# Two more stages of a decoder layer in seven products: query and key of heads 0 to 7, and a fourth pair in the recurrent output

## The chip, the cores and the metric

The kernel runs on one core of a Trainium2 chip, in one launch. The metric is the device time of that core in microseconds (us), the median of repeated runs. The profiled execution is one such run, recorded with every instruction. TensorE multiplies matrices and writes PSUM (8 banks of 128 x 512 fp32 values here), VectorE and ScalarE work element by element, GpSimd (POOL) issues the loads that add into their target, and SyncE (SP) issues the plain loads and stores.

## The reference

One layer of a decoder, 256 tokens, width 2048, all float32. `x` is normed and projected by one wide matrix; a recurrent branch and a stick-breaking attention run side by side, are gated and merged, and a feed-forward part and a gated embedding follow:

```
h = rmsnorm(x, g_mix)
x_r, g_r, q, k, v, gate_r, gate_a = split(h @ w_in)
y_r = gelu(g_r) * rg_lru(conv(x_r))          # 2816 wide
y_r = y_r @ w_rnn_out                        # 2816 -> 2048
q, k = head_rmsnorm(q), head_rmsnorm(k)      # 16 heads of 128
y_a = stick_breaking_attention(q, k, v) @ w_attn_out
x = x + (sigmoid(gate_r) * y_r + sigmoid(gate_a) * y_a) @ w_o
g, u = split(rmsnorm(x, g_ffn) @ w_ffn_gu)
x = x + (silu(g) * u) @ w_ffn_down           # 5632 wide
x = x + sigmoid(rmsnorm(x, g_ple) @ w_ple_gate) * (p @ w_ple_proj)
```

## The kernel before

**Numbers in two parts.** TensorE is used in its fp32r format. To keep precision, each operand is split into a high part and the rest (`whi`, `wlo` for weights). ScalarE writes the high part (line 370) and VectorE the rest (line 371). A *product*, `prod` (lines 640 to 644), is three matmuls of 512 columns: high by high, high by rest, rest by high.

**Weights.** `plan` lists all weight tiles in the order of use, cut into chunks of up to 1024 columns (512 KB). `Stream` loads them (line 281, on SP's queue, in the fixed order `DMA_ORDER`, each load behind the one before), sums them where asked, and splits them (lines 370 and 371). Split weights have five buffers, raw plain ones four (`w`), and everything else that is 1024 columns wide shares 31 buffers, tag "Q": normed inputs, recurrent outputs, attention's tiles, and the raw weights that take part in sums. Tiles of 512 columns share 18 buffers, tag "H". `need` keeps the splits four chunks ahead of the product that uses them, and sums two chunks more.

**Groups.** Stages from the recurrent output on compute two 128-token halves by two column blocks of 512 at once. `group` (line 706) runs such a group through a list of *slots*. A number is a plain chunk, one contraction tile of 128: 4 products. The other slots form the seven-product scheme for 2 x 2 blocks (Strassen's, in Winograd's form) over pairs of contraction tiles: "11", "T1", "21", "T2", "22", "T3", "T4" serve pairs 0 and 1 together, and A1 to A4 and B1 to B4 (written ("S", i, p)) serve pairs 2 and 3. Over all its slots a pair takes 7 products where the plain form takes 8. `pairs_of` says how many pairs a stage has: four for those named in `FOUR`, else three (two in the short last down part). The weights' sums are made by VectorE (line 292) and by loads that add into a tile (`joins`, line 330, issued by POOL). The inputs' sums come from `half_sums`: four operations of 128 columns and one split.

At a slot `group` can also run other work. The call's `also` names functions by slot, the list `todo` gives one to each slot from the second on, and the list `pend` (transposes of the stage just done) gives one to each slot in `TURNED_AT`. `whole` runs a group and adds its banks to the evacuated tiles, with four VectorE additions at its end.

**Blocks.** The present query and key projections and the attention gate use `block` (line 849): 512 columns, 16 contraction tiles, both token halves, 32 products. Every second contraction tile it calls `step`, eight steps a block. A step is four products.

**The order around the change.** Recurrence (11 channel pairs), recurrent output (two groups, slots `LONG`), value (two groups, `EVEN4`), then eight blocks Q0, K0, Q1, K1, ... and four gate blocks, which make 96 steps. Behind each query or key block stands `head_norms` (line 980): squares on ScalarE, a norm, and the scaled heads on VectorE. Attention for a pair of heads `hp` has four parts: `att_t` turns query and key by eight transposes, `att_z` makes the logits, `att_e` the sums along the keys and the weights, `att_o` the output. They are issued at steps 18 + 9 hp plus 0, 2, 7 and 11. The value tiles of the second value group are split by `next_v` at steps 1, 3, 5 and 7. At steps 93 to 95 `parts_sums` makes the input sums of the attention output, which follows. In the end come three rounds of gated groups (`gu`) and down parts (`dn`). The last down part has two groups with the slots `TWELVE`, and the stage behind it, `pg`, reads their result turned by `next_h` (line 1179).

**Scheduling.** The program fixes the order on each engine when it is built, by priorities in the order of the code and a time model. Waits between engines are semaphores.

Of the kernel before, what the change touches and what calls it, by code (L numbers as in the profile page):

```python
# [32 lines left out]
A1, A2, A3, A4 = [("S", i, 2) for i in (1, 2, 3, 4)]  # L33
B1, B2, B3, B4 = [("S", i, 3) for i in (1, 2, 3, 4)]
FIRST3 = ["11", A1, 6, "T1", A2, 7, "T2", "21", "22", A3, "T3", 8, A4, 9, "T4", 10, 11, 12, 13, 14, 15]
EVEN3 = ["11", A1, 6, "T1", A2, 7, "21", 8, "T2", 9, "22", A3, 10, "T3", 11, A4, 12, "T4", 13, 14, 15]
EVEN4 = ["11", A1, 8, B1, "T1", 9, A2, B2, 10, "21", "T2", 11, "22", A3, 12, B3, "T3", 13, A4, B4, 14, "T4", 15]
LONG = ["11", 6, A1, 7, "T1", 8, A2, 9, "T2", 10, "21", 11, "22", 12, A3, 13, "T3", 14, A4, 15, "T4",
        16, 17, 18, 19, 20, 21]
TWELVE = [("S", 1, 0), ("S", 1, 1), 4, ("S", 2, 0), 5, ("S", 2, 1), 6, ("S", 3, 0), 7, ("S", 3, 1), 8, ("S", 4, 0), 9,  # L40
          ("S", 4, 1), 10, 11]
TWO = (0, 1)
FOUR = ("gu", "v")
LAST_GROUP = ("pg", 1)
W_BUFS = 4
RAW_AHEAD = 12.0
SUMS_AHEAD = 2
TURNED_AT = {"first": (5, 7, 9, 11), "twelve": (6, 8, 10, 12), "even": (9, 11, 13, 15)}
NEG = -1e30


def pairs_of(name):

    if name[:2] == "dn":
        q = int(name[2])
        return [FQ0[q] // 2 + i for i in range(3 if FQ[q] == 16 else 2)]
    return (0, 1, 2, 3) if name in FOUR else (0, 1, 2)


def is_sum(x):  # L60

    return isinstance(x, str) or isinstance(x, tuple) and x[0] == "S"
# [14 lines left out]
C_XR, C_GR, C_Q, C_K, C_V, C_GTR, C_GTA = 0, 22, 44, 60, 76, 92, 108  # L77
# [3 lines left out]
NPC = 226  # L81


ATT_AT = (0, 2, 7, 11)


def rg_k_tiles(j):
# [77 lines left out]
def tail():  # L165


    def wide(name, w, slots, c=0):
        return [(name, g, w, c + 8 * g, c + 8 * g + 4, slots[g]) for g in range(2)]

    def blocks(*cs):
        return [("blk", b, None, c, None, None) for c, b in cs]

    def gu(*gs):
        return [("gu", g, "gu", 4 * g, 44 + 4 * g, EVEN4 if g else FIRST3) for g in gs]

    def dn(q):
        k, p = FQ0[q], FQ0[q] // 2
        slots = [x + k if isinstance(x, int) else (*x[:2], x[2] + p) if isinstance(x, tuple) else x
                 for x in (EVEN3 if FQ[q] == 16 else TWELVE)]  # L180
        return wide(f"dn{q}", "dn", [slots] * 2)

    x = [("x", 0), ("x", 1)]
    return (wide("ro", "ro", [LONG] * 2) + wide("v", "in", [EVEN4] * 2, C_V)
            + blocks(*[(c, b) for b in range(4) for c in (C_Q, C_K)], *[(C_GTA, b) for b in range(4)])
            + wide("ao", "ao", [EVEN3] * 2) + wide("wo", "wo", [FIRST3, EVEN3]) + gu(0, 1, 2, 3) + dn(0) + gu(4, 5, 6, 7) + dn(1)
            + gu(8, 9, 10) + dn(2)
            + wide("pg", "pg", [FIRST3[:-4] + x + FIRST3[-4:]] * 2))
# [234 lines left out]
def tile_hybrid_block(ctx: ExitStack, tc: tile.TileContext, xT: bass.AP, x: bass.AP, pT: bass.AP,  # L423
# [12 lines left out]
    def tl(tag, dt=F32):  # L436
        cnt[0] += 1
        tag = "H" if tag in "CT" else "Q"
        n, c = NT[tag]
        return act.tile([P, c], dt, tag=tag, name=f"{tag}_{cnt[0]}", bufs=n)  # L440

    def psum():
        cnt[0] += 1
        return pps.tile([P, 512], F32, tag="ps", name=f"ps_{cnt[0]}")

    def f32(ap):
        return ap.bitcast(F32)

    def tt(o, a, b, op):
        nc.vector.tensor_tensor(o, a, b, op)  # L450

    def stt(o, a, s, b, op0, op1):
        nc.vector.scalar_tensor_tensor(o, a, s, b, op0, op1)

    def actv(o, i, f, **kw):
        nc.scalar.activation(o, i, f, **kw)  # L456
# [27 lines left out]
    def pc(base, j):  # L484
        return prm_sb[:, base + j:base + j + 1]
# [37 lines left out]
    def parts(t):  # L523
        v = t.rearrange("p (e x s) -> p e x s", e=2, x=2)
        return v[:, :, 0, :], v[:, :, 1, :]

    def pair(t):
        return t.rearrange("p (e s) -> p e s", e=2)
# [105 lines left out]
    pend, todo = [], []  # L634

    def tok(pairs, k, t):
        x = rhs(pairs, k)
        return x[:, t * P:t * P + P], x[:, 256 + t * P:384 + t * P]

    def prod(ps, x, wh, wl, start=False, stop=False, goes_on=False):  # L640

        nc.tensor.matmul(ps, x[0], wh, start=start, stop=False, skip_group_check=goes_on)  # L642
        nc.tensor.matmul(ps, x[0], wl, start=False, stop=False, skip_group_check=goes_on)  # L643
        return nc.tensor.matmul(ps, x[1], wh, start=False, stop=stop, skip_group_check=goes_on)  # L644
# [39 lines left out]
    xg = []  # L684
# [21 lines left out]
    def group(at, pairs, sums, after=None, also=()):  # L706
# [8 lines left out]
                 if isinstance(x, int) or is_sum(x)]  # L715
        turned_at = TURNED_AT["twelve" if len(slots) == len(TWELVE) else
                              "first" if slots[2] == 6 and slots[8] == "22" else "even"]
# [49 lines left out]
    xc, xcs, gel, y, gtr, ysum, xsum = {}, {}, {}, [], [], {}, {}  # L767
# [81 lines left out]
    def block(c0, b, step=None):  # L849

        pss = [psum() for _ in range(2)]
        wt = S_.take(("blk", c0, b))
        for k in range(KD):
            if step is not None and k % 2 == 0:
                step()
            _, _, hi, lo, o = wt[4 * k]
            for t, ps in enumerate(pss):
                prod(ps, tok(xg, k, t), hi[:, o:o + 512], lo[:, o:o + 512], k == 0, k == KD - 1)
        return pss

    def rs_x(t):
        return rstd_tok[:, t:t + 1]
# [7 lines left out]
    @contextmanager  # L870
    def behind_splits():
        with tc.issue_after(S_.hi_ins.ins), tc.issue_after(S_.lo_ins.ins):
            yield
# [15 lines left out]
    pss = group(("gtr", 0), xg, None, None, also)[0]  # L889
# [12 lines left out]
    for p in range(NPR):  # L902
# [14 lines left out]
        def step():  # L917
            if count[0] in (0, 2, 4, 5):
                with behind_splits(), tc.issue_after(gelu.ins):
                    next(parts_, None)  # L920
            count[0] += 1

        pss = block(C_GTR, GATE_R_AT[p], step)
# [5 lines left out]
    def whole(at, pairs, sums, also=()):  # L929

        (q2, q4, q3, q8), t = group(at, pairs, sums, None, also)
        cs = [t[y] for y in ("11", "T3", "T2", "T1")]
        for c, q in zip(cs, (q2, q4, q3, q8)):
            tt(c, q, c, ALU.add)
        return cs

    def parts_sums(pairs, sums, p):
        h = tl("T")
        hi, lo = parts(pairs[p])
        tt(pair(h), f32(hi), f32(lo), ALU.add)  # L940
        sums[p] = half_sums(h)
# [8 lines left out]

    n = len(LONG)
    for g in range(2):
# [9 lines left out]
    def next_v():  # L962
        c, r = vc.pop(0), rs_x(len(vs) % 2)
        v = tl("B", F32R)
        actv(v[:, :512], c, AF.Identity, scale=r)
        stt(v[:, 512:], c, r, f32(v[:, :512]), ALU.mult, ALU.subtract)
        vs.append(v)
# [5 lines left out]
    qs, ks, zst, ost = {}, {}, {}, []  # L973
# [3 lines left out]

    heads = {C_Q: {}, C_K: {}}

    def head_norms(c0, b, step):  # L980

        pss = block(c0, b, step)
        ss = stat.tile([P, 16], F32, tag="ss", name=f"ss_{c0}_{b}")
        for t, ps in enumerate(pss):
            q = tl("T")
            for h in range(4):
                actv(q[:, h * P:h * P + P], ps[:, h * P:h * P + P], AF.Square, scale=rs_x(t),
                     accum_out=ss[:, 4 * t + h:4 * t + h + 1])
        r = ss[:, 8:]
        rsqrt_mean(r, ss[:, :8], HD)  # L990
        for t, ps in enumerate(pss):
            nc.vector.tensor_scalar(r[:, 4 * t:4 * t + 4], r[:, 4 * t:4 * t + 4], rs_x(t), None, ALU.mult)
            c = tl("T")
            tt(c.rearrange("p (h d) -> p h d", h=4), ps.rearrange("p (h d) -> p h d", h=4),
               r[:, 4 * t:4 * t + 4].unsqueeze(2).to_broadcast([P, 4, P]), ALU.mult)
            heads[c0][b, t] = c
# [14 lines left out]
    def att_t(hp):  # L1011
        ks[hp] = turn_heads(C_K, hp, pc(PC_KG, 0))
        qs[hp] = turn_heads(C_Q, hp, qg)
# [73 lines left out]

    at = {}
    for hp in range(NHP):
        for d, f in enumerate(ATT_AT):  # L1090
            at.setdefault(18 + 9 * hp + f, []).append(((att_t, att_z, att_e, att_o)[d], hp))
    osum = {}
    for i, p in enumerate(pairs_of("ao")):
        at[93 + i] = [(lambda p: parts_sums(ost, osum, p), p)]
    slot = [0]

    def step():
        for f, hp in at.pop(slot[0], ()):
            f(hp)
        slot[0] += 1  # L1100

    for b in range(4):
        if b == 0:
            for i in range(4):
                at.setdefault(1 + 2 * i, []).append((lambda _: next_v(), 0))
        head_norms(C_Q, b, step)
        head_norms(C_K, b, step)
    gta = []
    for b in range(4):
        pss = block(C_GTA, b, step)  # L1110
# [87 lines left out]
    for g in range(2):  # L1198
# [5 lines left out]
        for n, ps in enumerate(group(("wo", g), mix, msum, onto_x1(g))[0]):  # L1204
            t, b = n % 2, 2 * g + n // 2
# [77 lines left out]
    for g in range(2):  # L1283
        qs_, t_ = group(("pg", g), h3, sum3, also={len(FIRST3) - 4: embedded(g)} | (
            {} if g else {10: lambda: token_scales(1, rs2)}))
        for n, (q, c) in enumerate(zip(qs_, ("11", "T3", "T2", "T1"))):
            t, b, op = n % 2, 2 * g + n // 2, ALU.add
            c, ps, o = t_[c], pp.pop(0), tl("T")
# [76 lines left out]
```

## Time and profile before

| | |
|---|---|
| median of 3 runs | 1856.9 us (1856.87 to 1857.93) |
| profiled execution | 1856.98 us, of which the span from first to last instruction is 1855.2 us |
| VectorE, ScalarE busy | 1499.7 us (81%), 1253.4 us (68%) |
| loaded | 409.11 MB, mean 221 GB/s |

The page gives busy times, the span in 40 slices, the chain of work that ended last, and groups of instructions by line. In a group's row, "| 851.6, 390 | 0.2 <-" means busy us in total, mean ns of one, and the idle time of the engine just before it with what ended it. In rows by time, the first two numbers are start and length in us, and a bracket gives the idle time before it and its releaser.

### The profile page before, as it was taken

What the parts mean: (1) busy time and instruction counts of PE and PEld (TensorE: products, weight loads), DVE (VectorE), ACT (ScalarE), POOL (GpSimd) and SP (SyncE); (2) the same over time, 40 slices, a digit from 0 to 9 for tenths busy, and PEclk for the clock granted to TensorE, in tenths of its full rate; (3) what the DMA queues carried; (4) which work ended last, traced back from release to release, by engine and by line L of the source; (5) the groups of instructions that cost most, each with busy time, mean ns of one, the idle gap of its engine ahead of it and who ended that gap; (6) DMA issues with size and microseconds to landing.
All of it is one profiled execution on the core that took longest, in us unless ns stands there. A gap on an engine that the chain in (4) does not pass through costs nothing.

```text
span 1855.2 us, 24724 instructions
## 1 busy us (share of the span) xinstructions
PE 1845.1 (99%) x8885; PEld 1552.7 (84%) x8885; DVE 1499.7 (81%) x1889; ACT 1253.4 (68%) x1679; POOL 115.9 (6%) x140
## 2 busy tenths in 40 slices
PE   9999999999999999999999999999999999999998
PEld 7899889888888888888888888888888888888787
DVE  7688887677888576667799889888799988898986
ACT  7687888774565566667566677665576655666774
POOL 0000000000010000000000011100111101110100
PEclk9999999999999999999999999999999999999999
DMA  8555556577786544556787788888888878887674
GB/s 295 176 178 188 191 188 199 200 234 240 250 248 188 191 167 145 173 162 225 227 253 236 224 258 235 245 246 255 250 261 254 233 239 247 251 252 231 207 238 141
DMA packets 121082, 409.11 MB, mean 221 GB/s; under 512 B 13568, under 2 KB 14208, under 8 KB 120960
## 3 DMA queue, kind: packets, MB, share of 16 engines
q1 hardware_dynamic: 101808, 359.82, 54.9%
q0 software_dynamic: 19008, 47.72, 15.1%
q8 instruction: 69, 1.13, 0.2%
q14 instruction: 53, 0.43, 0.1%
q10 hardware_dynamic: 144, 0.01, 0.0%
HBM read 405.40 MB, written 2.10 MB: 220 GB/s over the span
## 4 chain that ended last, share of the span: by engine, by line
PE 97%; DVE 1%; DMA 0%; issue 0%; ACT 0%; SPq 0%; ACTq 0%; DVEq 0%
PE ps L643 26%; PE ps L642 26%; PE ps L644 26%; PE ps L572 9%; PE ps L576 5%; PE ps L556 1%; PE ps L555 1%; PE ps L554 1%; DVE H L450 1%; PE ps L1233 1%; DVE wlo L371 0%; PE ps L1003 0%; DMA w<-in_w_dram 0%; PE ps L1176 0%; ACT whi L370 0%
## 5 line engine op out<-in xcount | busy, mean ns | idle before, releaser
L643 PE MATMUL ps<-wlo,Q 128*128 128x512 f32 x2185 | 851.6, 390 | 0.2 <-DVE wlo L371 0.2
L644 PE MATMUL ps<-whi,Q 128*128 128x512 f32 x2185 | 849.6, 389 | 0.0
L642 PE MATMUL ps<-whi,Q 128*128 128x512 f32 x2185 | 772.0, 391 | 2.0 <-ACT whi L370 2.0
L371 DVE TENSOR_TENSOR wlo<-w,whi 128x1024 fp32r<-128x1024 f32 (+2 forms) x498 | 598.8, 1208 | 203.7 <-ACT whi L370 198.8
L370 ACT ACTIVATE whi<-w 128x1024 fp32r<-128x1024 f32 (+2 forms) x498 | 518.5, 1047 | 246.4 <-PE ps L644 190.8
L642 PEld LDWEIGHTS ps<-whi,Q 128*128 128x128 f32 x2185 | 409.9, 188 | 87.0 <-ACT whi L370 3.4
L644 PEld LDWEIGHTS ps<-whi,Q 128*128 128x128 f32 x2185 | 410.3, 188 | 84.7
L643 PEld LDWEIGHTS ps<-wlo,Q 128*128 128x128 f32 x2185 | 410.4, 188 | 84.0 <-DVE wlo L371 0.5
L370 ACT ACTIVATE whi<-Q 128x1024 fp32r<-128x1024 f32 (+1 forms) x339 | 339.1, 1006 | 209.4 <-PE ps L644 188.5
L371 DVE TENSOR_TENSOR wlo<-Q,whi 128x1024 fp32r<-128x1024 f32 (+1 forms) x339 | 389.4, 1157 | 68.0 <-ACT whi L370 66.0
L330 POOL DMA_DIRECT2D Q<-in_w_dram x132 | 113.4, 863 | 1690.9 <-DVE Q L292 532.6
L572 PE MATMUL ps<-Q,whi 128*128 128x512 f32 x704 | 170.7, 392 | 0.0
L572 PEld LDWEIGHTS ps<-Q,whi 128*128 128x128 f32 x704 | 128.8, 188 | 24.5
L456 ACT ACTIVATE H<-ps 128x512 f32<-128x512 f32 (+1 forms) x171 | 89.4, 537 | 52.6 <-PE ps L644 41.4
L292 DVE TENSOR_TENSOR Q<-Q,Q 128x512 f32<-128x512 f32 (+1 forms) x132 | 115.9, 888 | 10.5 <-DMA Q<-in_w_dram 10.1
L450 DVE TENSOR_TENSOR H<-H,H 128x512 f32<-128x512 f32 (+1 forms) x208 | 116.8, 573 | 2.0 <-ACT H L456 1.5
L450 DVE TENSOR_TENSOR H<-ps,H 128x512 f32<-128x512 f32 (+1 forms) x154 | 88.5, 604 | 17.5 <-PE ps L644 12.2
L576 PEld LDWEIGHTS ps<-Q,wlo 128*128 128x128 f32 x704 | 90.4, 191 | 3.5
L576 PE MATMUL ps<-Q,wlo 128*128 128x256 f32 x704 | 91.5, 283 | 0.0
L456 ACT ACT_TABLE_LOAD x53 | 68.0, 1283 | 1.7 <-DVE Q L450 0.7
L456 ACT ACTIVATE Q<-H 128x512 fp32r<-128x512 f32 x69 | 42.2, 626 | 35.7 <-DVE H L450 35.1
L450 DVE TENSOR_TENSOR Q<-H,Q 128x512 fp32r<-128x512 f32 (+1 forms) x77 | 52.4, 685 | 0.8 <-ACT Q L456 0.7
(122 smaller groups left out, 890.6 us busy)
## 6 DMA issues: line engine op xcount, KB each, us to landing
w<-in_w_dram SPq DMA_DIRECT2D x473, 512.0 KB, 4.2
Q<-in_w_dram SPq DMA_DIRECT2D x182, 512.0 KB, 6.0
Q<-in_w_dram POOLq DMA_DIRECT2D x50, 512.0 KB, 6.6
Q<-in_w_dram POOLq DMA_DIRECT2D x82, 256.0 KB, 5.2
w<-in_w_dram SPq DMA_DIRECT2D x16, 448.0 KB, 3.3
H<-in_x_dram SPq DMA_DIRECT2D x8, 256.0 KB, 7.8
H<-in_xT_dram SPq DMA_DIRECT2D x7, 256.0 KB, 5.6
out_dram<-H SPq DMA_DIRECT2D x7, 256.0 KB, 2.9
```

Source lines behind the costliest of these rows:

```text
L292: add = lambda o, a, b: self.nc.vector.tensor_tensor(o, a, b, ALU.add)
L330: self.nc.gpsimd.dma_start(t[:, c:], src[:, a:a + 1024 - c], accum_op=ALU.add)
L370: self.hi_ins = self.nc.scalar.activation(h[:, q], t[:, q], AF.Copy)
L371: self.lo_ins = self.nc.vector.tensor_tensor(l[:, q], t[:, q], h[:, q].bitcast(F32), ALU.subtract)
L450: nc.vector.tensor_tensor(o, a, b, op)
L456: nc.scalar.activation(o, i, f, **kw)
L554: nc.tensor.matmul(o, wt[0], xh, start=start, stop=False)
L572: nc.tensor.matmul(pss[e], wt[0], rhs(xs, k), start=(k == 0), stop=(k == n - 1))
L576: nc.tensor.matmul(pss[e][:, :256], wt[1], rhs(xs, k)[:, :256], start=False, stop=False)
L642: nc.tensor.matmul(ps, x[0], wh, start=start, stop=False, skip_group_check=goes_on)
L643: nc.tensor.matmul(ps, x[0], wl, start=False, stop=False, skip_group_check=goes_on)
L644: return nc.tensor.matmul(ps, x[1], wh, start=False, stop=stop, skip_group_check=goes_on)
```

## The change

Five things are changed.

- The recurrent output gets a fourth pair: "ro" joins `FOUR`, and `LONG` starts its plain chunks at 8 instead of 6 and has B1 to B4 in it. With that the recurrence also makes `half_sums` for channel pair 3.
- The blocks Q0, K0, Q1 and K1 become two groups ("qk", 0) and ("qk", 1) with four pairs and the slots `EVEN4`. Group b computes four heads' queries and keys together. `head_norms` takes finished tiles, writes the heads back into them, and is put on `todo`: the norms of group 0 run at slots 1 and 2 of group 1, those of group 1 at steps 0 and 1 of the blocks behind. The blocks of heads 8 to 15 stay.
- The value's `next_v` moves from the steps to slots 3, 5, 7 and 9 of the first new group.
- Attention is laid over 64 steps instead of the steps 18 to 95. `att_t` of head pairs 0 and 1 is issued at slots 17 and 19 of the second new group, the others at the steps of `TURN_AT`. `att_z`, `att_e` and `att_o` come 2, 7 and 11 steps behind `ATT_FROM`: head pairs are 7 or 8 steps apart where they were 9. `parts_sums` comes at steps 61 to 63.
- In the last down part the transposes on `pend` are issued at slots 4, 6, 8 and 10 instead of 6, 8, 10 and 12.

```diff
-LONG = ["11", 6, A1, 7, "T1", 8, A2, 9, "T2", 10, "21", 11, "22", 12, A3, 13, "T3", 14, A4, 15, "T4",
-        16, 17, 18, 19, 20, 21]
+LONG = ["11", 8, A1, 9, B1, "T1", 10, A2, 11, B2, "T2", 12, "21", 13, "22", A3, 14, B3, "T3", 15, A4, 16, B4, 17, "T4",
+        18, 19, 20, 21]
...
-FOUR = ("gu", "v")
+FOUR = ("gu", "v", "ro", "qk")
...
-TURNED_AT = {"first": (5, 7, 9, 11), "twelve": (6, 8, 10, 12), "even": (9, 11, 13, 15)}
+TURNED_AT = {"first": (5, 7, 9, 11), "twelve": (4, 6, 8, 10), "even": (9, 11, 13, 15)}
...
-ATT_AT = (0, 2, 7, 11)
+ATT_AT = (2, 7, 11)
+ATT_FROM = (-1, 6, 14, 21, 29, 36, 43, 51)
+TURN_AT = (None, None, 8, 12, 25, 30, 42, 49)
...
-            + blocks(*[(c, b) for b in range(4) for c in (C_Q, C_K)], *[(C_GTA, b) for b in range(4)])
+            + [("qk", b, "in", C_Q + 4 * b, C_K + 4 * b, EVEN4) for b in range(2)]
+            + blocks(*[(c, b) for b in (2, 3) for c in (C_Q, C_K)], *[(C_GTA, b) for b in range(4)])
...
-    def head_norms(c0, b, step):
-
-        pss = block(c0, b, step)
+    def head_norms(c0, b, pss, outs=None):
...
-            c = tl("T")
+            c = outs[t] if outs else tl("T")
...
     for hp in range(NHP):
+        if TURN_AT[hp] is not None:
+            at.setdefault(TURN_AT[hp], []).append((att_t, hp))
         for d, f in enumerate(ATT_AT):
-            at.setdefault(18 + 9 * hp + f, []).append(((att_t, att_z, att_e, att_o)[d], hp))
+            at.setdefault(ATT_FROM[hp] + f, []).append(((att_z, att_e, att_o)[d], hp))
...
-        at[93 + i] = [(lambda p: parts_sums(ost, osum, p), p)]
+        at.setdefault(61 + i, []).append((lambda p: parts_sums(ost, osum, p), p))
...
     def step():
+        if todo:
+            todo.pop(0)()
...
-    for b in range(4):
-        if b == 0:
-            for i in range(4):
-                at.setdefault(1 + 2 * i, []).append((lambda _: next_v(), 0))
-        head_norms(C_Q, b, step)
-        head_norms(C_K, b, step)
+    for b in range(2):
+        cs = whole(("qk", b), xg, xsum, {17: lambda: att_t(0), 19: lambda: att_t(1)} if b else {
+            3 + 2 * i: next_v for i in range(4)})
+        for c0, c in ((C_Q, cs[:2]), (C_K, cs[2:])):
+            todo.append((lambda c0, b, c: lambda: head_norms(c0, b, c, c))(c0, b, c))
+    for b in (2, 3):
+        for c0 in (C_Q, C_K):
+            head_norms(c0, b, block(c0, b, step))
```

## The prediction

> **What bounds the kernel now.** I read the page first (busy shares, slices, chain), then the order of time on the engines, then windows by stage.
>
> ```profile
> span 1855.2 us, 24724 instructions
> ...
> PE 1845.1 (99%) x8885; PEld 1552.7 (84%) x8885; DVE 1499.7 (81%) x1889; ACT 1253.4 (68%) x1679; POOL 115.9 (6%) x140
> ...
> PE 97%; DVE 1%; DMA 0%; issue 0%; ACT 0%; SPq 0%; ACTq 0%; DVEq 0%
> ...
> L371 DVE TENSOR_TENSOR wlo<-w,whi 128x1024 fp32r<-128x1024 f32 (+2 forms) x498 | 598.8, 1208 | 203.7 <-ACT whi L370 198.8
> L370 ACT ACTIVATE whi<-w 128x1024 fp32r<-128x1024 f32 (+2 forms) x498 | 518.5, 1047 | 246.4 <-PE ps L644 190.8
> L642 PEld LDWEIGHTS ps<-whi,Q 128*128 128x128 f32 x2185 | 409.9, 188 | 87.0 <-ACT whi L370 3.4
> ...
> Q<-in_w_dram SPq DMA_DIRECT2D x182, 512.0 KB, 6.0
> ```
>
> TensorE is busy 99% of the span, and 97% of the chain that ended last is its own. ScalarE waits to split weights until TensorE frees a buffer (190.8 us of its idle time stand against TensorE), so the splits run ahead. The question is therefore what TensorE issues, and where it waits. Its waits over the whole run, and the issue spacing:
>
> ```profile
> PE ps L642 <- ACT whi L370: 2.0, 3, 1.4
> PE ps L491 <- DVE H L488: 1.6, 1, 1.6
> PE ps L643 <- DVE wlo L371: 0.2, 1, 0.2
> ```
>
> ```profile
> 639.46 0.39 PE L642 MATMUL ps<-whi,Q 128*128 128x512 f32 x1
> 639.68 0.39 PE L643 MATMUL ps<-wlo,Q 128*128 128x512 f32 x1
> 639.91 0.39 PE L644 MATMUL ps<-whi,Q 128*128 128x512 f32 x1
> 640.14 0.39 PE L642 MATMUL ps<-whi,Q 128*128 128x512 f32 x1
> ```
>
> All named waits come to 3.8 us. The first start and the fourth are 0.68 us apart, 0.227 us for each matmul of 512 columns; the 0.39 us shown overlap. A product, the kernel's unit (`prod`, three matmuls), thus costs **0.68 us** of the end time.
>
> On this the Trainium skill (page "Perfetto Trace Analysis", section "Identifying the Most-Contended Engine") says that matmul busy time overstates how full TensorE is, and that the share of weight loads is the better measure. Here that share is 84%, which would leave a sixth free and price a removed matmul nearer its 0.188 us load; 30 of them would then give 5.6 us. The spacing of 0.227 us without waits decides against it: this case's trace does not bear that headroom out.
>
> **The change part by part.** I counted `L642` through the plan to find where stages begin.
>
> *Products.* A pair of contraction tiles takes 8 products plainly and 7 by the scheme. The recurrent output gets a fourth such pair in each of 2 groups: 85 products become 84, minus 2 in all. Query and key of heads 0 to 7 were four blocks of 32 products; they become two groups of 4 pairs, 2 x 60 instead of 2 x 64, minus 8. Ten products, 30 matmuls: 10 x 0.68 = **6.8 us removed**. Transposes and attention matmuls keep their number.
>
> *What feeds the recurrent output.* Per group two plain chunks go, and three chunks of 1024 and one of 512 come: 1.5 splits more (1.2 us VectorE, 1.05 ScalarE each), two sums of 512 and two accumulating loads on POOL's queue. That is about 3.2 us of VectorE and 1.6 of ScalarE a group. The fourth pair's half sums, made once in the recurrence, add some 2 us of VectorE, an estimate by the split row (five instructions that pass 1024 columns in all). The busier of the two groups:
>
> ```profile
> 447.70:505.50 57.80, 57.80 (x257) 47.86 (x255) 48.23 (x66) 32.29 (x35) 3.42 (x4) 1.00 0.73 235
> 505.50:544.50 39.00, 39.00 (x174) 32.30 (x173) 33.77 (x36) 24.81 (x27) 4.27 (x5) 1.00 0.82 250
> 544.50:585.30 40.80, 40.80 (x182) 33.78 (x181) 36.12 (x39) 26.95 (x32) 5.27 (x6) 1.00 0.67 184
> 630.60:885.60 255.00, 255.00 (x1266) 215.74 (x1265) 173.50 (x242) 175.76 (x312) 1.71 (x2) 1.00 0.53 175
> 1350.30:1392.00 41.70, 41.70 (x189) 34.53 (x188) 39.19 (x50) 29.41 (x36) 4.32 (x5) 1.00 0.89 252
> ```
>
> Columns: stretch, length, then busy us of TensorE, weight loads, VectorE, ScalarE and POOL, clock, DMA share, GB/s. The first row (second recurrent group) goes from 48.2 of 57.8 to 51.4 of 57.1 us, 0.90. The last row, a later group of the same four-pair form, runs at 0.94 without a wait. Cost: 0.
>
> *The query-key groups.* The value groups (rows two and three) have the same slots. The first query-key group carries four `next_v` like the second value group: 0.89. The second drops those and takes two head norms and two turnings (`att_t` 0 and 1), which I price by these rows of the present stretch:
>
> ```profile
> L450 DVE TENSOR_TENSOR H<-ps,ss 128x512 f32<-128x512 f32 x16 | 10.3, 683 | 0.0
> ...
> L453 DVE SCALAR_TENSOR_TENSOR Q<-ps,prm_sb,Q 128x512 fp32r<-128x512 f32 x8 | 6.0, 745 | 0.0
> ...
> L992 DVE TENSOR_SCALAR ss<-ss,rstd_tok 128x4 f32<-128x4 f32 x16 | 2.8, 223 | 0.0
> ```
>
> ```profile
> 608.38 0.37 ACT L456 ACTIVATE H<-ps,rstd_tok 128x128 f32<-128x128 f32 x1 [0.98 <-PE ps L644]
> ...
> 611.14 1.10 ACT L370 ACTIVATE whi<-w 128x1024 fp32r<-128x1024 f32 x1
> ```
>
> VectorE: 36.1 - 4 x 0.745 (a `next_v` passes the same 512 columns) + 4 x (0.68 + 0.22) + 4 x 0.745 = 39.7 us in 40.8 us of products plus some 1.7 us of transposes: 0.93, again below the group at 0.94. ScalarE: a head norm holds splits up from 608.38 to 611.14, 2.8 us, and two stand one behind the other at the start of this group and again at steps 0 and 1 behind it. Five buffers of split weights cover that: at the group's start four chunks hold ten products, 6.8 us, against 5.6 us and a split. The margin is thin, so a wait can appear. From below it is zero (the present groups of this form have none); from above I take the 2.8 us of one uncovered norm. I take **+0.5 us**, since what precedes it is no fuller than rows that run clean. The turnings read heads normed over 20 us before, so the products queued behind them on TensorE do not wait long.
>
> *Attention closer together.* Row four covers 80 steps, with 80 x 2.72 = 218 us of products and 37 of attention. The new stretch has 64 steps: 174 + 36 = 210 us. VectorE loses 16 splits (19.6), one norm and two turnings: 149 of 210, 0.71 where it was 0.68. ScalarE: 176 - 17 - 3.3 - 2.7 = 153, 0.73 where it was 0.69. Logits still lie 5 steps before the sums and 9 before the outputs, so TensorE asks no sooner than now. No added cost. The sums for the attention output keep their place, the last three steps.
>
> *Transfers.* Each query-key group adds two accumulating loads of 512 KB and four of 256 KB, each recurrent group two of 256 KB: 5 MB in all, and 16 more issues on a POOL that is 6% busy. In the stretch concerned the rate rises from 175 GB/s towards the 250 of the value groups, which ran without a wait. Hidden by that room; without it each late load would cost the wait priced under the slower rival. SP's loads keep their number.
>
> *Transposes sooner.* The last down part precedes the one long wait inside the kernel:
>
> ```profile
> 1729.67 0.60 PE L1176 MATMUL ps<-ident,H 128*128 128x128 f32 x4
> ...
> 1741.78 0.60 PE L1176 MATMUL ps<-ident,H 128*128 128x128 f32 x4
> ```
>
> ```profile
> 1752.77 0.48 DVE L453 SCALAR_TENSOR_TENSOR Q<-ps,prm_sb,Q 128x256 fp32r<-128x256 f32 x1
> ...
> 1753.76 1.82 DVE L292 TENSOR_TENSOR Q<-Q,Q 128x1024 f32<-128x1024 f32 x2
> ```
>
> ```profile
> 1757.26 1.06 ACT L370 ACTIVATE whi<-Q 128x1024 fp32r<-128x1024 f32 x1 [0.94 <-DVE Q L292]
> ```
>
> ```profile
> 1756.54 0.40 PE L642 MATMUL ps<-whi,Q 128*128 128x512 f32 x1
> 1758.37 0.50 PE L642 MATMUL ps<-whi,Q 128*128 128x512 f32 x1 [1.44 <-ACT whi L370]
> ```
>
> TensorE starts at 1758.37 what could start at 1756.77: 1.6 us lost. It waits for a split, that for weight sums (`L292`), and those stand on VectorE among the leavings of the four transposes issued from 1729.67 to 1741.78 (`L453` at 1752.77 is one of them). Two slots sooner is a plain chunk and two products, 4.1 us, so some 2 us of that work leave the queue ahead of the sums. I take **1.5 us gained**, between 0 (the load, not VectorE, is late) and 1.6. What is late next is the sum behind these, whose user comes later still. In the first half of this part the two turnings of the last gated group also come two slots sooner; their input is ready here:
>
> ```profile
> 1689.54 0.75 DVE L453 SCALAR_TENSOR_TENSOR H<-H,rs,H 128x512 f32<-128x512 f32 x1
> ```
>
> It ends at 1690.3, the slot begins at 1683.8 + 10 products = 1690.6: no wait, at most a few tenths.
>
> **Sum.** The profiled execution took 1856.98 us, 1.8 around its span; the median, 1856.9, is the same. 1856.98 - 6.8 - 1.5 + 0.5 = **1849.2 us**.
>
> **The rivals.**
>
> *The wait before the last stage stays.* If the sums are held by their loads or the scheduler puts the transposes elsewhere, 1.5 us are not gained: 1850.7. Against it: VectorE ran `L292` at 1753.76 right behind other work, not behind a landing.
>
> *The second query-key group and the steps behind it run into ScalarE and VectorE.* If two norms in a row exhaust the four chunks once in the group and again at steps 0 and 1, each costs a norm less a part of the margin, some 2 us: 4 us in place of 0.5, 1852.7. For it: 0.93 on VectorE with ScalarE bursts, which no present group combines. Against it: the rows at 608.38 and 611.14, where a norm was taken with no wait on TensorE.
>
> *Slower: weight tiles run out of buffers.* The 31 wide buffers hold in the recurrent output 8 normed inputs, 11 outputs and now 4 half sums, 23; the four-pair form wants 8 or 9 weight tiles where the old wanted 6 or 7. SP issues in a fixed order, so one load without a buffer holds all behind it. If in all of the four new groups one load falls out of its lead, each costs landing and split, 6.0 + 1.05 + 1.2 = 8.3 us less what is covered; at half, 4 x 4.1 = 16.6 us, 1856.98 - 7.8 + 16.6 = 1865.8. It decides once a load is held some 10 us. Against it, SP's present waits: nearly all are for the small `w` buffers, and the last wide tiles for the recurrent output are asked for before that stage begins at 389.9:
>
> ```profile
> SPq L281 <- DVE wlo L371: 1348.5, 434, 11.0
> ```
>
> ```profile
> 388.11 1.28 SPq L281 DMA_DIRECT2D Q<-in_w_dram  x2
> ```
>
> The Trainium skill (same page, section "Identifying Performance Opportunities") says that a gap that repeats on the engine that should be full can mean missing room for the next tile; this trace has no such gap on TensorE, and no run shows yet what 23 held buffers do.
>
> **How the numbers follow.** Forecast 0.62, first rival 0.13, second 0.13, slower 0.12. A measurement here can tell about 0.2%, 3.7 us: faster means below 1853.2. The first three lie there, save a third of the second, which passes that bound: 0.83 faster, 0.06 same with that third and the milder cases of the fourth, 0.11 slower. The forecast's own range is 1848.3 to 1850. Downward, the two waits of TensorE on ScalarE that are left, 0.6 us by the wait row, could vanish by new timing: 1847.8. Upward it takes in the first two rivals and a little beyond: 1855.
>
> **What would show it.** Thirty fewer `L642` to `L644` matmuls at 0.227 us; TensorE's waits on `whi` no longer holding the 1.4 us near the last stage; transposes `L1176` in the last down part some 4 us nearer its start; VectorE near 0.93 in the second query-key group. New waits of TensorE on `whi` or `wlo` in the recurrent or query-key groups, or on attention's lines, would make the prediction wrong, and SP waiting for wide tiles would name the slower rival.

## The result, and the profile after

| | changed kernel | kernel before |
|---|---|---|
| median | 1852.82 us (16 runs, 1851.56 to 1855.29) | 1856.97 us (16 runs) |
| ratio | 0.9977, 95% interval 0.9969 to 0.9984 | |
| profiled execution | 1853.49 us, span 1851.8 us | 1856.98 us, span 1855.2 us |
| loaded | 414.37 MB | 409.11 MB |

The change saves 4.15 us where 7.7 were forecast. The time lies in the upper half of the range given (1847.8 to 1855), but outside the forecast's own range of 1848.3 to 1850. Two single runs at a lower granted clock, 2221.89 us of the kernel before and 3099.54 us of the variant with both turnings mended and earlier loads, are left out of the ratios and of that variant's median. The page after, first the engines, then the three matmuls of a product (lines are shifted by three: 645 to 647 are the old 642 to 644, 373 and 374 the split, 295 the weight sums, 453 the helper `tt`):

```profile
PE 1840.3 (99%) x8855; PEld 1545.9 (83%) x8855; DVE 1535.0 (83%) x1940; ACT 1272.1 (69%) x1705; POOL 128.9 (7%) x156
...
L646 PE MATMUL ps<-wlo,Q 128*128 128x512 f32 x2175 | 848.5, 390 | 0.8 <-DVE wlo L374 0.8
```

TensorE has 8855 matmuls instead of 8885. The 30 are gone, 6.8 us at 0.227 us each. Of these, 3.5 us arrived in the profiled execution, and the rest went into new waits. What TensorE waited for over the whole run:

```profile
PE ps L645 <- ACT whi L373: 2.5, 7, 0.6
PE ps L494 <- DVE H L491: 1.6, 1, 1.6
PE ps L646 <- DVE wlo L374: 0.8, 3, 0.4
PE ps L645 <- DVE Q L453: 0.5, 1, 0.5
```

Columns: us in total, times, longest. The 1.4 us wait of before is gone from the list, but there are 12 waits instead of 5. (The 1.6 us on `L494` lies at the very start of the kernel, before the first matmul, in every profile.) I placed the others by looking for matmul starts further apart than 0.227 us. Lost time in us, in the order of the stages: first the waits, then in brackets what single matmuls beside them took longer:

```
                                   before   changed
first value group, 11 us in          0           1.5 (0.55)
first query-key group, 15 us in      0           0.6 (0.1)
start of a key block (heads 8-11)    0           0.6 (0.1)
first gated group                    0.9 (0.2)   0.9 (0.2)
start of the last stage              1.6 (0.1)   1.2 (0.3)
```

The busy times of the stages, by windows (columns as in the prediction: length, TensorE, weight loads, VectorE, ScalarE, POOL, clock, DMA share, GB/s):

```profile
447.00:504.20 57.20, 57.20 (x254) 47.34 (x254) 48.29 (x65) 33.75 (x37) 4.26 (x5) 1.00 0.76 236
504.20:545.30 41.10, 40.11 (x174) 31.97 (x173) 36.64 (x40) 24.40 (x27) 5.12 (x6) 1.00 0.85 249
586.10:627.60 41.50, 41.07 (x181) 33.63 (x180) 37.38 (x40) 27.34 (x32) 5.22 (x7) 1.00 0.86 253
627.60:672.30 44.70, 44.70 (x205) 36.83 (x204) 40.73 (x49) 33.97 (x68) 4.30 (x5) 1.00 0.67 182
672.30:882.70 210.40, 209.86 (x1058) 178.05 (x1057) 149.77 (x219) 152.62 (x274) 1.58 (x2) 1.00 0.53 175
```

They are the second recurrent group, the first value group, the two query-key groups and the 64 steps of attention. On the average of its stage, none is at its limit on VectorE or ScalarE. The losses are local, and each has to be looked at in its place.

**The first value group.** VectorE's order of time as the stage begins, in the changed kernel:

```profile
500.99 1.21 DVE L374 TENSOR_TENSOR wlo<-w,whi 128x1024 fp32r<-128x1024 f32 x1
504.24 0.69 DVE L295 TENSOR_TENSOR Q<-Q,Q 128x512 f32<-128x512 f32 x1 [2.04 <-DMA Q<-in_w_dram]
504.85 0.68 DVE L453 TENSOR_TENSOR H<-ps,H 128x512 f32<-128x512 f32 x1
```

and in the kernel before, 505.5 being the stage's start there:

```profile
502.64 0.69 DVE L292 TENSOR_TENSOR Q<-Q,Q 128x512 f32<-128x512 f32 x1
503.25 0.68 DVE L450 TENSOR_TENSOR Q<-H,Q 128x512 fp32r<-128x512 f32 x1
```

Here the weight sum stands 2.04 us for its load and holds the rest of VectorE's list behind it: the group's four additions, the last of the value stage's input sums, splits. VectorE has no room to make this up: from 506 to 520 us it is busy 13.95 of 14 us, and 14.0 in the kernel before, so its share of 0.89 over the whole stage hides a full stretch. TensorE reaches the gap 11 us into the stage:

```profile
516.14 0.50 PE L646 MATMUL ps<-wlo,Q 128*128 128x512 f32 x1 [0.23 <-DVE wlo L374]
517.89 0.74 PE L645 MATMUL ps<-whi,Q 128*128 128x512 f32 x2 [0.56 <-ACT whi L373]
518.84 1.20 PE L645 MATMUL ps<-whi,Q 128*128 128x512 f32 x4 [0.21 <-ACT whi L373]
```

**The start of a key block.** TensorE, then VectorE:

```profile
697.81 1.03 PE L1005 MATMUL ps<-ident,H 128*128 128x128 f32 x8
699.39 0.50 PE L645 MATMUL ps<-whi,Q 128*128 128x512 f32 x1 [0.54 <-DVE Q L453]
```

```profile
698.32 0.43 DVE L453 TENSOR_TENSOR ps<-ps,negt 128x256 f32<-128x256 f32 x1
698.65 1.01 DVE L453 TENSOR_TENSOR Q<-Q,ps 128x512 f32<-128x512 f32 x2
```

At step 8 the logits of pair 1, the sums of pair 0 and the turning of pair 2 come together with a new block that wants two banks. The releaser named is the operation that reads the sums' bank (`Q<-Q,ps`).

**The start of the last stage.** The loss is now in three pieces, where the kernel before had one of 1.6 us:

```profile
1754.12 0.50 PE L646 MATMUL ps<-wlo,Q 128*128 128x512 f32 x1 [0.16 <-DVE wlo L374]
1755.87 0.73 PE L645 MATMUL ps<-whi,Q 128*128 128x512 f32 x2 [0.33 <-ACT whi L373]
1756.82 0.96 PE L645 MATMUL ps<-whi,Q 128*128 128x512 f32 x3 [0.21 <-ACT whi L373]
```

The turnings of the last down part stand at 1726.11 and 1727.24, and then at 1735.7 and 1736.8:

```profile
1726.11 0.60 PE L1185 MATMUL ps<-ident,H 128*128 128x128 f32 x4
1727.24 0.60 PE L1185 MATMUL ps<-ident,H 128*128 128x128 f32 x4
```

The second down group starts at 1715.0 us here and at 1717.9 before, counted by the products that follow. From there the turnings stand 11.1, 12.2, 20.7 and 21.8 us in; before the change it was 11.8, 18.0, 20.0 and 23.9. So the second came 5.7 us sooner, the fourth 2.1, the first 0.7, and the third came 0.7 us later. The slots did come 4.1 us sooner, but by the code a turning is also held behind the last product of the slot before (`issue_after(mm_)`). At slots 4, 6, 8 and 10 that is a product in bank "B", which waits until ScalarE has evacuated the partial sum standing there.

### The profile page after: what moved, and what is told of

The parts are those of the page before. It is cut to its first block, busy times and chain, and to the rows that moved or that the text cites. A ratio compares the mean times of both kernels' runs of the same rounds, so it can differ in the third digit from the quotient of the medians.

```text
span 1851.8 us, 24810 instructions
## 1 busy us (share of the span) xinstructions
PE 1840.3 (99%) x8855; PEld 1545.9 (83%) x8855; DVE 1535.0 (83%) x1940; ACT 1272.1 (69%) x1705; POOL 128.9 (7%) x156
## 2 busy tenths in 40 slices
DMA packets 123388, 414.37 MB, mean 224 GB/s; under 512 B 13824, under 2 KB 14464, under 8 KB 123264
## 4 chain that ended last, share of the span: by engine, by line
PE 96%; DVE 2%; DMA 1%; issue 0%; ACT 0%; SPq 0%; ACTq 0%; DVEq 0%
PE ps L645 26%; PE ps L646 26%; PE ps L647 26%; PE ps L575 9%; PE ps L579 5%; PE ps L558 1%; PE ps L559 1%; PE ps L557 1%; DVE wlo L374 1%; DVE H L453 1%; PE ps L1242 1%; DVE Q L295 0%; ACT whi L373 0%; PE ps L1185 0%; PE ps L1005 0%
## 5 line engine op out<-in xcount | busy, mean ns | idle before, releaser
L647 PE MATMUL ps<-whi,Q 128*128 128x512 f32 x2175 | 846.0, 389 | 0.0
L645 PE MATMUL ps<-whi,Q 128*128 128x512 f32 x2175 | 753.5, 391 | 3.0 <-ACT whi L373 2.5
L374 DVE TENSOR_TENSOR wlo<-w,whi 128x1024 fp32r<-128x1024 f32 (+2 forms) x478 | 574.0, 1206 | 167.9 <-ACT whi L373 163.5
L373 ACT ACTIVATE whi<-w 128x1024 fp32r<-128x1024 f32 (+2 forms) x478 | 497.0, 1046 | 223.0 <-PE ps L647 173.4
L373 ACT ACTIVATE whi<-Q 128x1024 fp32r<-128x1024 f32 (+1 forms) x377 | 376.4, 1004 | 212.6 <-PE ps L647 182.9
L374 DVE TENSOR_TENSOR wlo<-Q,whi 128x1024 fp32r<-128x1024 f32 (+1 forms) x377 | 431.1, 1152 | 58.0 <-ACT whi L373 54.1
L333 POOL DMA_DIRECT2D Q<-in_w_dram x148 | 126.8, 859 | 1674.9 <-DVE Q L295 583.2
L295 DVE TENSOR_TENSOR Q<-Q,Q 128x512 f32<-128x512 f32 (+1 forms) x148 | 128.2, 878 | 15.0 <-DMA Q<-in_w_dram 14.3
L453 DVE TENSOR_TENSOR H<-H,H 128x512 f32<-128x512 f32 (+2 forms) x214 | 119.8, 570 | 2.5 <-ACT H L459 1.9
L453 DVE TENSOR_TENSOR H<-ps,H 128x512 f32<-128x512 f32 (+1 forms) x162 | 93.3, 605 | 16.8 <-PE ps L647 12.0
L453 DVE TENSOR_TENSOR Q<-H,Q 128x512 fp32r<-128x512 f32 (+1 forms) x78 | 52.9, 682 | 0.8 <-ACT Q L459 0.7
```

The lines of the kernel that those rows point to most:

```text
L295: add = lambda o, a, b: self.nc.vector.tensor_tensor(o, a, b, ALU.add)
L333: self.nc.gpsimd.dma_start(t[:, c:], src[:, a:a + 1024 - c], accum_op=ALU.add)
L373: self.hi_ins = self.nc.scalar.activation(h[:, q], t[:, q], AF.Copy)
L374: self.lo_ins = self.nc.vector.tensor_tensor(l[:, q], t[:, q], h[:, q].bitcast(F32), ALU.subtract)
```

## The experiments

Each is the changed kernel with one edit, except where said. The changed kernel itself gave 1852.8 at first and 1852.0 in a later series, and its single runs lie up to 3.7 us apart, so differences under 1 us are read from the profiles' waits and not from the medians.

**Transposes back at their old slots.**

```diff
-"twelve": (4, 6, 8, 10)
+"twelve": (6, 8, 10, 12)
```

> The changed kernel with the last down part's transposes back at slots 6, 8, 10 and 12. Theory: the sooner slots bought almost nothing, because each transpose is also held behind the last product of the slot before, and at these slots that product stands in the shared bank that waits for its evacuation; so 1852.8 plus 0.2, about 1853.0 us, with TensorE losing 1.4 to 1.6 us in one piece near the start of the last stage. Rival (as predicted): the sooner slots are worth 1.5 us, and this run takes 1854.3 us.

1852.31 us (1851.29 to 1853.59), no slower than the changed kernel. In its profile the start of the last stage again lost 1.6 us in one piece, against 1.2 in three. The sooner slots are worth 0.4 us of waits in the profile (0.2 with the slower matmuls beside them) and nothing that the times show; the rival is out.

**The recurrent output with three pairs again.**

```diff
-LONG = ["11", 8, A1, 9, B1, "T1", 10, A2, 11, B2, ...
+LONG = ["11", 6, A1, 7, "T1", 8, A2, 9, "T2", ...
-FOUR = ("gu", "v", "ro", "qk")
+FOUR = ("gu", "v", "qk")
```

> The changed kernel with the recurrent output back at three pairs and its old slots. Theory: the fourth pair's sums and loads push the first value group's raw loads some 3 us nearer to their use and fill VectorE at the end of the second recurrent group, and the 2.1 us that TensorE loses some 11 us into the first value group come from that; they go, two products (1.4 us) come back, so about 1852.1 us. Rival: the loss has another source (the new order of the stages behind it); it stays, and the time is 1854.2 us.

1852.10 us, as the theory had it. TensorE's waits in its profile:

```profile
PE ps L494 <- DVE H L491: 1.6, 1, 1.6
PE ps L645 <- ACT whi L373: 1.1, 4, 0.4
PE ps L645 <- DVE Q L453: 0.5, 1, 0.5
PE ps L646 <- DVE wlo L374: 0.2, 1, 0.2
```

Behind the start of the kernel, all that is left lies at the key block, at the first gated group and at the last stage. In the value and query-key groups no matmul starts more than 0.12 us late. So the fourth pair of the recurrent output brought the loss in the value group, and at this setting it gave back about the 1.4 us that its two products saved.

**Transposes behind plain chunks.**

```diff
-"twelve": (4, 6, 8, 10)
+"twelve": (5, 7, 9, 11)
```

> The changed kernel with the last down part's transposes at slots 5, 7, 9 and 11, behind plain chunks, whose banks wait for no evacuation. Theory: they then stand 3 to 12 matmuls sooner in TensorE's order at three of four places than in the kernel before, VectorE's work is spread, and about half or more of the 1.2 us near the start of the last stage goes: 1851.7 to 1852.2 us. Rival: VectorE is full there whatever the order, and nothing changes: 1852.8 us.

1851.61 us. The turnings now stand evenly, 4.6 to 5 us apart:

```profile
1724.74 0.60 PE L1185 MATMUL ps<-ident,H 128*128 128x128 f32 x4
1729.76 0.60 PE L1185 MATMUL ps<-ident,H 128*128 128x128 f32 x4
1734.32 0.60 PE L1185 MATMUL ps<-ident,H 128*128 128x128 f32 x4
1738.89 0.60 PE L1185 MATMUL ps<-ident,H 128*128 128x128 f32 x4
```

The loss at the last stage fell from 1.2 to 0.4 us of waits. One slot later than the change has it is better than the change: what counts is which product a turning is pinned to, and not the number of its slot. (This profile also shows a wait of 0.9 us in the second value group, which the edit does not touch. VectorE stood still 1.19 us for a load 17 us before it.)

**Head pair 2 turned two steps later.**

```diff
-TURN_AT = (None, None, 8, 12, 25, 30, 42, 49)
+TURN_AT = (None, None, 10, 12, 25, 30, 42, 49)
```

> The changed kernel with the turning of head pair 2 at step 10 instead of 8. Theory: at step 8 a new block, the turning and the logits of head pair 1 all want banks at once, and the 0.7 us that TensorE loses there waiting for VectorE to release a bank of the sums go: 1852.1 us. Rival: VectorE's backlog behind the two norms is the cause; the wait stays or moves, 1852.8 us.

1852.23 us. The 0.7 us at the key block are gone:

```profile
PE ps L645 <- ACT whi L373: 2.4, 7, 0.6
PE ps L494 <- DVE H L491: 1.6, 1, 1.6
PE ps L646 <- DVE wlo L374: 0.4, 2, 0.2
```

No wait on `DVE Q L453` is left, and none has come up elsewhere in attention.

**The value stage's input sums spread.** They move from the last four slots of the second recurrent group to slots 19, 21, 23 and 25.

```diff
-also = {n - 4 + i: (lambda p: lambda: parts_sums(xg, xsum, p))(p) ...
+also = {n - 10 + 2 * i: (lambda p: lambda: parts_sums(xg, xsum, p))(p) ...
```

> The changed kernel with the four input sums for the value groups spread over slots 19, 21, 23 and 25 of the second recurrent group instead of its last four. Theory: VectorE stands still 2.04 us for a late raw load and then has the last of these sums, the group's four additions and the new stage's sums at once; with the sums done before, the standstill costs nothing, the 1.5 us of waits some 11 us into the first value group and the half us of slower pairs around them go: about 2 us less than the changed kernel's 1852.8, 1850.8 us. Rival (late load): the sums behind the load wait as long as before, TensorE's waits stay, 1852.8 us.

1851.41 us (1850.92 to 1851.66). The theory's place was right and its size too large: the loss in the value group fell to a wait of 0.3 us (0.4 with the matmul beside it). VectorE's standstill for the load went as well, since the sum that had waited now stands 5 us later in VectorE's order, at 509.61 us. So this run does not separate the crowd of sums from the late load.

**Raw loads 16 us ahead.**

```diff
-RAW_AHEAD = 12.0
+RAW_AHEAD = 16.0
```

> The changed kernel with the loads for weight sums placed 16 us ahead in the fixed order instead of 12. Rival (late load): the raw loads of the first value group land some 3 us earlier against the stage, VectorE does not stand still, the waits there go, 1850.8 us or, with better leads elsewhere, less. Theory (burst of sums): the standstill goes, but the crowd on VectorE remains and with it part of the waits, about 1852 us. Either way, more wide tiles are held at a time; if these run out, SP waits on them and the time rises over 1853.5.

1849.12 us (1848.75 to 1849.90), ratio to the kernel before 0.9959 (0.9946 to 0.9972). What VectorE waited for from 447 to 520 us, in the changed kernel and here:

```profile
DVE wlo L374 <- ACT whi L373: 6.6, 8, 2.3
DVE Q L295 <- DMA Q<-in_w_dram: 2.0, 1, 2.0
```

```profile
DVE wlo L374 <- ACT whi L373: 8.0, 8, 2.3
```

No standstill for a load in this stretch, and no wait of TensorE in any value or query-key group, without a move of the sums. VectorE's list around this seam (the border between two stages) is in the same order as in the changed kernel, and as full. So the late load is what decided there. The other profiles bear this out. Six are of kernels that are alike up to this point; the load's lateness differs from one to the next, and TensorE's loss follows it one to one (us, waits and slower matmuls together):

```
                              VectorE's standstill   TensorE's loss
changed kernel                        2.04                2.05
head pair 2 two steps later           1.90                1.82
transposes behind plain chunks        1.72                1.71
changed kernel once more              1.62                1.65
transposes at their old slots         1.00                1.05
both turnings mended                  0.77                0.82
three pairs; raw loads at 16          none                none
```

The losses at the first gated group went too, and that at the last stage fell to 0.5 us. A wait of 0.6 us came up in the output projection.

**Both turnings mended, and both with the spread sums.**

> The changed kernel with both mends of the turnings: last down part at slots 5, 7, 9 and 11, head pair 2 at step 10. Theory: the two add, 0.8 + 0.7 us less in the profile, 1851.3 us. Rival (one gap only moves into another): 1852.2 or more.

> All three together: last down part at slots 5, 7, 9 and 11, head pair 2 at step 10, input sums of the value groups spread. Theory: what the prediction left out is all in these three places, so this comes near the forecast of 1849.2, at 1849.3 to 1850 us. Rival: 1851.3, if the sums are not the cause in the first value group.

1850.07 us (1849.57 to 1852.31) and 1850.35 us (1849.62 to 1850.75). The two turnings add up; what lies beyond that is within the scatter. The spread sums add nothing to them in the median: in the first of the two profiles the value group lost only 0.6 us anyway, 0.3 in the second. The forecast of the first was beaten by 1.2 us, that of the second missed by 0.4.

**Both turnings mended, raw loads 16 us ahead.**

> The changed kernel with both mends of the turnings and the loads for weight sums 16 us ahead. Theory: the two sets of waits are separate, so the 0.7 us at the block's start and part of the 0.5 us before the last stage go on top of what the earlier loads gave: 1849.1 - 0.7 - 0.3 = 1848.1 us. Rival: the earlier loads have used up the room and nothing is added, 1849.1 us.

1848.86 us in the median of four runs, 1848.71 in the profiled execution, ratio 0.9955 (0.9942 to 0.9969): the best version run. The wait at the key block is gone. At the last stage nothing improved, 0.6 us against 0.5, so the slots behind plain chunks help there only at the shorter lead, and the gain over the earlier loads alone is within the scatter.

**The kernel before with raw loads 16 us ahead.**

> The kernel before with the loads for weight sums 16 us ahead. Theory: it had no waits in the value groups and can win only the 0.9 us at the first gated group and part of the 1.6 us before the last stage, so 1855.2 to 1856.3 us; the distance to the changed kernel with the same lead is then 6 to 7 us, close to the products removed. Rival: earlier loads are worth 3.7 us to any kernel of this form, 1853.2 us, and the changed kernel owes its loss nothing of its own.

Both missed: 1859.58 us, ratio 1.0013 (1.0004 to 1.0022), slower than with 12. The losses at the first gated group went, as in the changed kernel, but at the start of the last stage this happened:

```profile
1753.10 0.39 PE L644 MATMUL ps<-whi,Q 128*128 128x512 f32 x1
1756.15 1.90 PE L642 MATMUL ps<-whi,Q 128*128 128x512 f32 x5 [2.66 <-ACT whi L370]
1757.90 0.80 PE L643 MATMUL ps<-wlo,Q 128*128 128x512 f32 x1
1758.49 0.63 PE L644 MATMUL ps<-whi,Q 128*128 128x512 f32 x1
1758.92 0.63 PE L643 MATMUL ps<-wlo,Q 128*128 128x512 f32 x1
```

```profile
1756.00:1760.00 4.00, 3.85 (x10) 2.67 (x11) 4.00 (x5) 2.94 (x4) 0.85 (x1) 0.61 0.82 150
```

TensorE waited 2.66 us, and soon after ran at a mean granted clock of 0.61 for 4 us, with starts 0.43 us apart. The two together cost 4.6 us at the start of the last stage, where the kernel before loses 1.7. The longer lead is thus no gain in itself: it changes the fixed order everywhere, and each seam comes out anew. It suits the changed kernel, whose raw loads were late. Whether the old slots of the last down part are what it does not suit was not tested: no run has the kernel before with both the longer lead and other slots.

**The changed kernel once more.**

> The changed kernel once more, beside the two others on one chip, to measure distances without a change of chip: 1852.8 us by every theory, and waits in the first value group, at the block's start and before the last stage again, since they follow from the fixed order.

1851.99 us, beside 1857.12 for the kernel before. The waits in the value group, at the key block and at the last stage are there again, each within 0.2 us of the first profile. That in the first query-key group is not. It differs from run to run, and the traces show with what: as this group begins, VectorE stands still for a late load here too.

```profile
584.26 0.69 DVE L295 TENSOR_TENSOR Q<-Q,Q 128x512 f32<-128x512 f32 x1 [0.88 <-DMA Q<-in_w_dram]
```

TensorE loses time some 17 us later, and from 585 to 602 us VectorE is busy without a gap. In the six profiles of kernels that leave this stretch alone (us, counted as above):

```
                              VectorE's standstill   TensorE's loss
transposes at their old slots         1.74                1.50
changed kernel                        0.88                0.70
both turnings mended                  0.54                0.35
transposes behind plain chunks        0.49                0.31
head pair 2 two steps later           0.20                none
changed kernel once more              none                none
```

The loss is the standstill less some 0.2 us, so this is the cause found in the first value group once more, at the next border but one. With the loads 16 us ahead, a standstill of 1.26 us at this place cost 0.1 us. Why a load lands later in one run than in another was not settled.

## Why the prediction was right or wrong

- **Products.** Right. Thirty matmuls went, and their price of 0.227 us is what the windows show: the second recurrent group shrank from 57.8 to 57.2 us, and the sum below closes with it to 0.1 us. At 5.6 us for the thirty matmuls it would come out 1.1 us too long. The Trainium skill (page "Perfetto Trace Analysis", section "Identifying the Most-Contended Engine") says that the busy share of matmuls is not a good measure of how near TensorE is to its limit, and names the share of weight loads beside a second measure. That the busy share overstates is the prediction's reading of this. Here the share of weight loads hardly moved, from 83.7% to 83.5% of the span, and left no headroom.
- **Recurrent output, "Cost: 0".** This is the step that failed most. The busy time stayed below the estimate (48.3 us where 51.4 were reckoned; the first value group has 2.9 us more than before), and it didn't matter. The row that I took as a proof, a later group at 0.94 without a wait, speaks of VectorE's share. It says nothing on when the next stage's raw loads land against the place that its sums have in VectorE's fixed order. I looked at the transfers' rate and at SP's count of loads, not at their lead at the seam. The price was 2.05 us in the first profile and 0.8 to 1.8 in five others, against 1.4 us of products saved there. That the fourth pair brings it, and by a late load, is shown by the run with three pairs, by the run with earlier loads, and by the loss following the standstill from profile to profile. The 0.7 us of the first query-key group belong to the same step.
- **Query-key groups.** Right on the busy time (VectorE 40.7 us where 39.7 were reckoned, ScalarE no bound) and on the place that I feared: in the second group, with two norms in a row, TensorE never waited. The +0.5 us there was not needed. The wait in the first group, which I put at nothing, is between 0 and 1.4 us. It follows a late load as well.
- **Attention closer together.** The sums were right to a microsecond (VectorE 149.8 of 210.4 us, ScalarE 152.6). "No added cost" missed 0.7 us: I counted distances within one head pair, and not how many banks the coincidence at step 8 needs. Moving one turning by two steps gave it back. That it is the banks, and not VectorE's work, is read from the releaser in the rows above; the run itself does not tell the two apart.
- **Transposes sooner, "1.5 us gained".** Wrong, 0.2 to 0.4 us. The 4.1 us by which the slots moved were taken for the move of the transposes. `issue_after` pins them behind a product that waits for an evacuation, and the run at odd slots shows that with another product to stand behind, 1.2 us of the 1.6 us of waits can be had. My first rival, that the scheduler puts the transposes elsewhere, describes what happened. (The start of the first down group was misread too: by the count of products it is 1685.6 us and not 1683.8. There it only widens the margin.)
- **The second rival.** Its 1852.7 us lies next to the measured 1852.8 by accident. It asked for some 2 us in the second query-key group and as much at steps 0 and 1 behind it. TensorE waited at neither; what it lost behind them, 0.7 us at step 8, has another cause.
- **The slower rival.** It did not happen. SP's waits from 447 to 520 us did not grow, first before, then after:

```profile
SPq L281 <- DVE wlo L371: 53.6, 13, 8.6
SPq L281 <- DVE H L450: 11.4, 5, 4.4
```

```profile
SPq L284 <- DVE wlo L374: 48.9, 12, 10.4
SPq L284 <- DVE H L453: 9.2, 4, 3.2
```

  The 31 wide tiles held 23 long-lived ones and the four-pair form. Even the changed kernel with 16 us of lead, which by its order asks for tiles sooner, was faster.
- **The sum.** With the slower matmuls counted everywhere, 1856.98 - 6.8 + 2.05 + 0.7 + 0.7 - 0.2 = 1853.4, against 1853.49 in the profiled execution. Against the forecast, 1.3 us are missing at the transposes and 3 us are new waits beyond the 0.5 allowed. The median is 0.7 us below that execution. By the prediction's own signs of being wrong, new waits in a query-key group and on attention's lines, its account of the seams failed: the time fell into the stated range because that range reached up to the rivals.

## What to carry to other kernels

Where an engine is full, removed work was worth its issue time here, to 0.1 us in the sum. What was lost again was lost at the seams and where parts of the attention met: look at each place where the next stage's loads, sums and evacuations meet in one engine's order, and compare when each load lands with its place there. An average share of busy time below one proves nothing for such a place: 0.89 over a stage here held 14 us in which VectorE was full. When an instruction is moved by its place in the code, find what it is pinned behind, since that decides where it goes.

## What the runs showed of the hardware

In the kernel before with the longer lead, a wait of 2.66 us of TensorE (3.05 us from one matmul start to the next) was followed by a fall of the clock. It came 0.7 us after the first matmul behind the wait: from 1756.9 to 1760.3 us the granted clock was 0.50 (0.61 over the 4 us of the row above), with matmuls 0.43 us apart instead of 0.227. The wait of 1.44 us in the kernel before was not followed by one (starts 0.23 us apart from the second matmul on). Among the thirteen profiles this is the only wait inside the kernel above 1.5 us, and the only one with such a fall, so the link rests on one case. The Trainium skill ("TensorE: Matmul & The Clock Gate", section "Why this matters for your kernels") advises against idle gaps of more than about 3 us between matmuls because the clock falls back. Here a gap a little shorter was enough.

In six profiles, VectorE's standstill for one late load, 0.77 to 2.04 us, came back as a loss of TensorE of the same size, 0.82 to 2.05 us, some 11 to 13 us later. The same load of an unchanged stretch was late by a different time in each of them.
